# A two-layer decoder trunk in one core: weight sums, product order, buffers and transfers rescheduled by hand

## The chip, the cores and the metric

The kernel runs on one core of a Trainium2 chip. The metric is the device time of one execution in microseconds, the median of several runs; lower is better. The engines have short names in the profile: PE (TensorE, matmuls and transposes), PEld (its weight loads), DVE (VectorE), ACT (ScalarE), POOL (GpSimd), SP (SyncE). SP and POOL issue nearly all DMAs here.

## The reference, cut to what matters

The input x has 512 rows of 2048 columns, all float32. Layer 0 is forgetting attention (FoX) with 16 heads of 128, layer 1 is retention with 8 heads of 256 (keys) and 512 (values). Each layer is one input projection, the mixer, a SiLU gate and one output projection, and then a LayerNorm.

```python
def fox_branch(x, w_in, b_f, q_gain, k_gain, w_out):
    proj = einsum('bsd,de->bse', x, w_in)            # 2048 -> 4*2048 + 16
    q, k, v, gate, f_logit = split(proj, ...)
    q, k = rms_norm(heads(q), q_gain), rms_norm(heads(k), k_gain)
    c = cumsum(log_sigmoid(f_logit + b_f), axis=1)
    s = q @ k.T * scale + c[query] - c[key]          # causal
    o = softmax(s) @ v
    return (o * silu(gate)) @ w_out
def retention_branch(x, w_in, w_out):
    q, k, v, gate = split(x @ w_in, ...)             # 2048 -> 2*2048 + 2*4096
    q, k = rotary(q), rotary(k) * 256 ** -0.5
    o = causal (q @ k.T * decay) @ v, per head       # written in chunks
    return (group_norm_heads(o) * silu(gate)) @ w_out
def reference(x, ...):
    h = x
    for i in range(2):
        y = fox_branch(h, ...) if i == 0 else retention_branch(h, ...)
        h = layer_norm(ALPHA * h + y, ln_gain[i], ln_bias[i])
    return h
```

## The kernel before

**Products.** A float32 product is made of three matmuls of rounded parts: each operand is split into a high part and the rest, and `mm3` (lines 284 to 288) adds high x high, high x low and low x high. `split` (279 to 282) makes the high part on ScalarE (L281) and the low part on VectorE (L282). Weights come from DRAM as `w_raw` or `w_q` and are split on the way into `w_h` and `w_l`, three buffers each.

**Units and blocks.** A weight matrix is cut into units: 18 wide ones (1024 output columns) and 16 narrow ones (512). A unit is a 2 x 2 block product in Strassen's manner with seven products, p1 to p7; the sums of the left sides are the forms `a11`, `s1`, `s2` and so on. The right sides are sums of weight quarters. p1, p5, p6 and p4 share a chain: the quarter loaded first is `w_q`, and each of p5, p6 and p4 adds another quarter to it (L470, VectorE), to be split after that. p7's sum is L466. A product of a wide unit has 4 blocks of 12 matmuls of 128 x 512. The tables `ORDER`, `FIRST`, `REST` and `EARLY` give the order of the products, `blocks_of` unrolls them; within a group of two products the blocks alternate. W4 (output projection of layer 0, first half) and N8 (queries and keys of the first retention head) are plain products; W4's order is the table `HELD`, twelve of its 32 blocks use the split made for the block ahead of them (same weights, other rows).

**The planner.** Everything is issued in an order that class `Order` (83 to 215) finds while the program is built. All blocks of all units stand in one line. In a slot (`slot`) the planner loads weights up to nine blocks ahead, adds and splits two to three blocks ahead, and issues the block's matmuls. Before it adds block j it has split all blocks before j. Then it lets tasks go on. A task is a Python generator that yields what its next step needs: time on VectorE and ScalarE (`dve`, `act`), buffers ("rings": `mmp`, two PSUM buffers for everything but weights' products; `tmp`, `in0`, `g0`, `k0` and so on). A step goes in a slot only if the debts of both engines stay under `LIMIT`, 4.8 and 4.0 us; a slot pays off 2.7 to 2.8 us. When a block needs a buffer or a form that is not there (`require`), the planner forces tasks, whatever the debts, and so puts long chains into all queues at once. I call that a forced turn. Each engine executes its own queue strictly in that order.

**Tasks.** FoX (`Pair`, from 838): a pair of heads is projected in a narrow unit (N0 to N7), `normed` scales and transposes queries and keys (transposes L892, copies L886 and L887), `head` has eight turns of scores (L286 to L288 on `qk_h`), softmax (L931 to L953), transposes of the probabilities (L967), their copies `pT` (L922), products with the values (L998), transposes of the result (L1008). In each turn a step first copies what the turn ahead produced, frees its PSUM buffer, and then issues the next products. Heads go one after another, by `fox["heads"]`; they share the buffers g0, g1, g2 and d0. `to_columns` normalizes and transposes layer 0's output (L1241, copies L1229 and L1231). Retention (`Head`): N8 to N15 project queries and keys, W6 to W13 values and gates; `attend` makes rope (L1323 to L1327), scores and decay (L1355), `retain` the products with the values, the group norm (L1413 to L1430), the scaling by it (L1433), the gate's transposes (L1437), copies (L1444, L1445) and stores of the forms for the output projection. Those are fetched again by `fetch_form` for W14 to W17. In a unit, `keep` copies the sum of p1 into the buffer k0, which is free when the gates of the head ahead have been transposed.

**Transfers.** Weights and forms are loaded from SP's queue. W5 and W17 are run in the order `EARLY`: p7's and p4's weights are summed by DMAs that accumulate, from GpSimd's queue. `sum_ahead` (L399 to L407) issues all of p7's, four loads on SP and four accumulations on GpSimd, when p5 is done; right behind them in W17, `last_gains` (L1509 to L1512) issues two loads of 1 MB each, the last LayerNorm's gain and bias spread over all partitions.

Of the kernel before, what the change touches and what calls it, by code (L numbers as in the profile page):

```python
# [17 lines left out]
P = 128  # L18
# [25 lines left out]
def blocks_of(n, *groups):  # L44

    return [(p, c) for g in groups for c in range(n) for p in g]


FIRST = (("p1",), ("p2",))
REST = (("p5",), ("p6",), ("p3", "p7"), ("p4",))  # L50
ORDER = (("p1", "p5"), ("p6",), ("p3", "p7"), ("p2", "p4"))
# [7 lines left out]
        + [(2, 0, c, m) for c in range(4) for m in range(2)] + [(1, 1, c, 1) for c in range(4)]  # L59
        + [(2, 1, c, m) for c in range(4) for m in range(2)])  # L60
# [8 lines left out]
RINGS = dict(mmp=2, tmp=4, st=3, q=4, **{t: 1 for t in "k0 k1 k2 in0 in1 g0 g1 g2 d0 b0 b1 b2".split()})  # L69


LIMIT = 4.8, 4.0
# [10 lines left out]
class Order:  # L83
# [46 lines left out]
    def each(self, forced, rank):  # L130
        went = False
        for task in list(self.tasks):
# [8 lines left out]
            if not forced and any(d + c > most and c for d, c, most in zip(self.debt, cost, LIMIT)):  # L141
                continue
# [10 lines left out]
    time = 0.0  # L153

# [9 lines left out]
    def push(self, block):  # L164
        self.line.append(block)
        while len(self.line) - self.at > 9:
            self.slot()
# [11 lines left out]
    def slot(self):  # L179
# [22 lines left out]
        b.multiply()  # L202
        self.step()
# [19 lines left out]
def trunk(ctx: ExitStack, tc: tile.TileContext, xq, x, fb_f, columns, wf_in, narrow, wide, ln_g, ln_b, rot, decay,  # L223
# [80 lines left out]
    class Unit:  # L304
# [3 lines left out]
        def __init__(self, w, n, sink, rows=True, u2="k0"):  # L308
# [8 lines left out]
            self.kept_w = {}  # L317
# [17 lines left out]
        def keep(self, what, bank):  # L335
            n = self.shape[2]
            if self.wide or what == "u2":
                tag = {"p1": "k0", "p5": "k1", "u2": "k2"}[what] if self.wide else self.u2
# [27 lines left out]
        def after(self, p):  # L366
# [3 lines left out]
            if p == "p1":  # L370
                self.keep("p1", "x")
# [6 lines left out]
            if p == "p2":  # L378
# [20 lines left out]
        def sum_ahead(self):  # L399

            for i in range(2):
                t = pool.tile([P, 2, 2, 512], F32, name="v_sum", tag=HOME["s1"][i])
                for c in range(2):
                    self.summed["p7", 2 * i + c] = t[:, c]
                    d = t[:, c].rearrange("p a b -> p (a b)")
                    nc.sync.dma_start(d, self.source("12", 2 * i + c))
                    nc.gpsimd.dma_start(d, self.source("22", 2 * i + c), accum_op=ALU.add)  # L407
# [15 lines left out]
    class Block:  # L423
        before = None

        def __init__(self, unit, p, c, e, shares, shared, then_block, then_product):
# [15 lines left out]
            assert p != "p7" or shared or self.sums  # L442

# [139 lines left out]
    class PlainBlock:  # L583
        def __init__(self, unit, k, n, c, m, same, then, before, ahead):
            self.u, self.k, self.n, self.c, self.m = unit, k, n, c, m
            self.same, self.then, self.before, self.ahead = same, then, before, ahead
            self.done = False
            self.p = f"b{k}{n}"
# [119 lines left out]
    def fetch_form(i, name, tags, at=0, to=8):  # L708

        for c in range(at, to, 4):  # L710
            n = min(4, to - c)
            heads = 4 * i if i else c + n + (0 if name in ("a11", "a21", "s3") else 8)
            yield need(until=lambda: given[i > 0] >= heads and any(free[t] for t in tags))
# [10 lines left out]
            yield need(dve=dve(n * 256), act=act(n * 256), wait=3)  # L724
            split_form(name, t, c, c + n)
# [112 lines left out]
    class Pair:  # L838


        def __init__(self, i):
# [3 lines left out]
            self.rows_done = 0  # L845
# [20 lines left out]
        def normed(self):  # L866
# [10 lines left out]
            yield need(mmp=1, until=lambda: free["g0"] and free["g1"])  # L877
            take("g0")
            take("g1")
            self.qk = sb8("qk_h", "g0", F32R), sb8("qk_l", "g1", F32R)  # L880
            for s in range(ST + 1):
                if s:
                    yield need(act=0.85, dve=0.95, pe=0.45)
                    for i, gain in ((0, gq), (2, gk)):
                        h, l = (p[:, i:i + 2, (s - 1) * P:s * P] for p in self.qk)
                        nc.scalar.activation(h, t[:, i:i + 2], AF.Copy, scale=gain)  # L886
                        nc.vector.scalar_tensor_tensor(l, t[:, i:i + 2], gain, f32(h), op0=ALU.mult, op1=ALU.subtract)  # L887
                    give("mmp")
                if s < ST:
                    t = by4(mmp())  # L890
                    for h in range(4):
                        nc.tensor.transpose(t[:, h], raw[s][:, h * P:(h + 1) * P], ident)  # L892
# [5 lines left out]
        def head(self, i):  # L898
# [3 lines left out]
            yield need(d0=1, until=lambda: fox.get("forgot") and fox["heads"] == head)  # L902
            take("d0")
            cb = pool.tile([P, S], F32, name="cb", tag="d0")
# [5 lines left out]
            ps, p, tp = {}, {}, {}  # L910
            for t in range(8):
                wait = int(t > 0)
                if 5 <= t:
                    g = groups[t - 5]
                    yield need(act=sum(act(n_of(q)) for q in g), wait=wait, g2=int(t == 5))
                    wait = 0
                    if t == 5:
                        take("g2")
                        pT = sb8("pT", "g2")
# [20 lines left out]
                if 1 <= t < 4:  # L940
                    g = groups[t - 1]
                    yield need(act=sum(act(n_of(q)) for q in g), dve=sum(dve(n_of(q)) + 0.28 for q in g), wait=wait,
                               tmp=1)
                    wait = 0
                    b, at = tmp("p"), 0
# [12 lines left out]
                if t == 3:  # L958
                    give("d0")
                if 4 <= t < 7:  # L960
                    yield need(pe=0.45, wait=wait, mmp=1)
                    g = groups[t - 4]
                    tp[g] = by4(mmp())
                    at = 0
                    for q in g:
                        for k in range(q + 1):
                            nc.tensor.transpose(tp[g][:, at], p[q][0][:, k * P:(k + 1) * P], ident)  # L967
                            at += 1
                    give("tmp")
                if t < 3:  # L970
                    yield need(pe=0.7, wait=wait, mmp=1)
                    c, at = mmp(), 0
                    for q in groups[t]:
                        m = max(n_of(q), 256)
                        ps[q] = c[:, at:at + m]
                        at += m
                        mm3(ps[q], [x[:, i, q * P:(q + 1) * P] for x in self.qk], [x[:, 2 + i, :m] for x in self.qk],
                            True, True)
                    if t == 2:
                        if i:  # L980
                            give("g0")
                            give("g1")
                        else:
                            fox["heads"] = head + 1
# [14 lines left out]
            give("g2")  # L999
# [188 lines left out]
    def to_columns(m):  # L1188
# [24 lines left out]
        made = {}  # L1213
        for i in range(len(turns) + 2):
            yield need(dve=1.5 if m == 0 else 0.5, act=1.5, pe=0.45, mmp=int(i == 0))
            if 0 <= i - 2 and m == 0:
                s, c = turns[i - 2]
                es = slice(s % 2 * P, (s % 2 + 1) * P)
                k = c % 2 * 4
                split_form(f"a1{c // 2 + 1}", made.pop(i - 2), k, k + 4, es, s % 2 == 1)  # L1220
            if 0 <= i - 1 < 8:
                s, c = turns[i - 1]
                es = slice(s % 2 * P, (s % 2 + 1) * P)
                d = aq[f"{m + 1}{c // 2 + 1}"][:, c % 2 * 4:c % 2 * 4 + 4, es]
                for j in range(4):
                    k = c * 4 + j
                    g, b = cols[:, 2 + k:3 + k], cols[:, 2 + KT + k:3 + KT + k]
                    if j % (4 if m else 2) == 1:
                        nc.vector.tensor_scalar(d[:, j], ps[:, j], g, b, op0=ALU.mult, op1=ALU.add)  # L1229
                    else:  # L1230
                        nc.scalar.activation(d[:, j], ps[:, j], AF.Identity, scale=g, bias=b)  # L1231
                give("mmp")
                made[i - 1] = d
                if m and s % 2:
                    there.add((f"2{c // 2 + 1}", c % 2))
            if i < 8:
                s, c = turns[i]
                zs = z_part(s, c // 2)[:, c % 2 * 512:(c % 2 + 1) * 512]
                ps = by4(mmp())
# [347 lines left out]
```

## Time and profile before

| what | value |
|---|---|
| median of 3 runs | 2693.91 us (2693.76 to 2699.8) |
| profiled execution, its own time | 2688.65 us |
| its span, first to last instruction | 2686.9 us |
| mean granted clock of TensorE | 0.961 |
| busy: TensorE, VectorE, ScalarE, GpSimd | 2395.3, 1964.9, 1256.2, 212.4 us |
| moved by DMA | 482.71 MB, mean 180 GB/s |
| W4 and W5 (from the timeline) | 839 to 1105 us |
| retention's projections, N8 to W13 | 1105 to 2260 us |
| output projection, W14 to W17 | 2260 to 2660 us |

A wait in the profile names the instruction that waited, what ended the wait, the total in us, how often and the longest. In the timeline a row has start, duration, engine, line, operation, and in brackets the idle time of the engine ahead of it and what ended that. A row of the windows view has the busy time of each engine in a stretch, the granted clock (1.00 is full), the mean busy share of the 16 DMA engines and GB/s.

### The profile page before, as it was taken

Reading aid. Unit: us, or ns where it says so; the run is one execution under the profiler, and the core shown is the slowest. Engines: PE = TensorE matmul, PEld = TensorE weight load, DVE = VectorE, ACT = ScalarE, POOL = GpSimd, SP = SyncE. Lnnn points to the kernel's source line nnn. Section 1 sums busy time; section 2 is a strip of 40 time slices with the busy share of each in tenths; the row PEclk is TensorE's granted clock in tenths of the full one; section 3 lists DMA queues with packets and bytes.
Section 4 is the critical chain, followed back from the end, with each engine's and each line's share of the span. In section 5 each row is a group of like instructions: output and inputs, shape, how many; then the busy total and the mean of one; then the engine's idle time right before and its main releaser. Section 6 shows DMA issues by size and latency. Waiting matters only on the chain.

```text
span 2686.9 us, 34465 instructions
## 1 busy us (share of the span) xinstructions
PE 2395.3 (89%) x12964; PEld 2022.5 (75%) x12964; DVE 1964.9 (73%) x2551; ACT 1256.2 (47%) x1879; POOL 212.4 (8%) x316
## 2 busy tenths in 40 slices
PE   8889998998999697887889999999999998799975
PEld 8687787797798476776769797979797876577754
DVE  4768777667666255767778787878787878678758
ACT  4445566556556433553344444454444454434421
POOL 0000200110110101000010101010101010100010
PEclk9999999999999798999999999999999999899987
DMA  5344664664655368444465656565656566668682
GB/s 183 133 158 162 185 193 135 192 186 141 174 167 169 90 200 248 167 145 138 160 188 186 192 186 184 184 184 188 189 192 184 188 174 222 169 230 274 197 256 95
DMA packets 194487, 482.71 MB, mean 180 GB/s; under 512 B 19328, under 2 KB 71680, under 8 KB 194064
## 3 DMA queue, kind: packets, MB, share of 16 engines
q1 hardware_dynamic: 161872, 404.46, 45.5%
q0 software_dynamic: 32448, 76.04, 12.0%
q8 instruction: 102, 1.67, 0.2%
q14 instruction: 65, 0.53, 0.1%
HBM read 410.67 MB, written 69.76 MB: 179 GB/s over the span
## 4 chain that ended last, share of the span: by engine, by line
PE 26%; DVE 21%; ACT 7%; DMA 6%; issue 5%; SPq 0%; ACTq 0%; DVEq 0%
PE acc L287 8%; PE acc L286 8%; PE acc L288 8%; DVE w_l L282 7%; ACT w_h L281 5%; DVE w_q L470 5%; DMA w_raw<-in_wide 4%; DMA y_raw<-y_a 1%; DVE w_raw L466 1%; PE mmp L287 1%; PE mmp L288 1%; PE mmp L286 1%; DMA y_raw<-y_s 1%; DVE rope L1323 1%; DVE s L282 1%
## 5 line engine op out<-in xcount | busy, mean ns | idle before, releaser
L281 ACT ACTIVATE w_h<-w_q 128x1024 fp32r<-128x1024 f32 x384 | 403.4, 1058 | 665.3 <-DVE w_q L470 507.2
L282 DVE TENSOR_TENSOR w_l<-w_q,w_h 128x1024 fp32r<-128x1024 f32 x384 | 469.2, 1223 | 272.6 <-ACT w_h L281 269.9
L286 PE MATMUL acc<-w_h,s 128*128 128x512 f32 (+1 forms) x1536 | 575.9, 375 | 71.5 <-ACT w_h L281 48.6
L287 PE MATMUL acc<-w_l,s 128*128 128x512 f32 (+1 forms) x1536 | 576.5, 375 | 37.7 <-DVE w_l L282 37.3
L288 PE MATMUL acc<-w_h,s 128*128 128x512 f32 (+1 forms) x1536 | 564.2, 367 | 0.0
L286 PE MATMUL acc<-w_h,a 128*128 128x512 f32 (+1 forms) x1408 | 511.2, 363 | 37.3 <-ACT w_h L281 22.4
L282 DVE TENSOR_TENSOR w_l<-w_raw,w_h 128x1024 fp32r<-128x1024 f32 x324 | 394.4, 1223 | 203.1 <-ACT w_h L281 201.8
L287 PE MATMUL acc<-w_l,a 128*128 128x512 f32 (+1 forms) x1408 | 507.0, 360 | 3.6 <-DVE w_l L282 3.6
L281 ACT ACTIVATE w_h<-w_raw 128x1024 fp32r<-128x1024 f32 x324 | 339.3, 1054 | 358.2 <-DVE w_raw L466 183.2
L288 PE MATMUL acc<-w_h,a 128*128 128x512 f32 (+1 forms) x1408 | 505.3, 359 | 0.0
L286 PEld LDWEIGHTS acc<-w_h,s 128*128 128x128 f32 x1536 | 298.2, 194 | 129.6 <-ACT w_h L281 55.5
L287 PEld LDWEIGHTS acc<-w_l,s 128*128 128x128 f32 x1536 | 298.0, 194 | 115.3 <-DVE w_l L282 74.0
L470 DVE TENSOR_TENSOR w_q<-w_q,w_raw 128x1024 f32<-128x1024 f32 x280 | 341.7, 1220 | 35.2 <-DMA w_raw<-in_wide 32.4
L288 PEld LDWEIGHTS acc<-w_h,s 128*128 128x128 f32 x1536 | 298.0, 194 | 43.1
L286 PEld LDWEIGHTS acc<-w_h,a 128*128 128x128 f32 x1408 | 270.8, 192 | 77.5 <-ACT w_h L281 24.0
L287 PEld LDWEIGHTS acc<-w_l,a 128*128 128x128 f32 x1408 | 270.7, 192 | 45.1 <-DVE w_l L282 9.3
L288 PEld LDWEIGHTS acc<-w_h,a 128*128 128x128 f32 x1408 | 270.1, 192 | 38.3 <-DVE a L282 0.2
L286 PE MATMUL acc<-a,w_h 128*128 128x256 f32 x464 | 133.1, 287 | 10.6 <-ACT qk_raw L1298 10.4
L288 PE MATMUL acc<-a,w_l 128*128 128x256 f32 x464 | 132.3, 285 | 1.2 <-DVE w_l L282 1.2
L287 PE MATMUL acc<-a,w_h 128*128 128x256 f32 x464 | 132.1, 285 | 0.0
L286 PE MATMUL acc<-s,w_h 128*128 128x256 f32 x448 | 127.4, 284 | 3.1 <-ACT p L351 3.1
L288 PE MATMUL acc<-s,w_l 128*128 128x256 f32 x448 | 127.6, 285 | 0.1
(204 smaller groups left out, 2969.2 us busy)
## 6 DMA issues: line engine op xcount, KB each, us to landing
w_raw<-in_wide SPq DMA_DIRECT2D x360, 512.0 KB, 3.5
w_raw<-in_narrow SPq DMA_DIRECT2D x164, 512.0 KB, 3.5
w_q<-in_wide SPq DMA_DIRECT2D x68, 512.0 KB, 4.5
w_q<-in_narrow SPq DMA_DIRECT2D x28, 512.0 KB, 5.3
y_s<-ny POOLq DMA_DIRECT2D x48, 256.0 KB, 6.2
y_s<-y POOLq DMA_DIRECT2D x40, 256.0 KB, 4.1
y_raw<-y_s SPq DMA_DIRECT2D x32, 256.0 KB, 4.4
y_raw<-y_a SPq DMA_DIRECT2D x26, 256.0 KB, 4.6
```

Source lines behind the costliest of these rows:

```text
L281: nc.scalar.activation(h, src, AF.Copy)
L282: nc.vector.tensor_sub(l, src, f32(h))
L286: nc.tensor.matmul(ps, a[0], b[0], start=start, stop=False, skip_group_check=True)
L287: nc.tensor.matmul(ps, a[0], b[1], start=False, stop=False, skip_group_check=True)
L288: nc.tensor.matmul(ps, a[1], b[0], start=False, stop=stop, skip_group_check=True)
L466: nc.vector.tensor_add(self.t, self.t, u.lent.pop(("p3", c)))
L470: nc.vector.tensor_add(u.chain[c], u.chain[c], t)
L1323: nc.vector.tensor_mul(a, raw[j], cos[:, None, :].to_broadcast([P, 2, 512]))
```

## The change

1. **Sums ahead.** A block now has `follows`: the place in the line of the block that the same chain was last summed for (p1 for p5, p5 for p6, p6 for p4). Before a sum the planner splits only up to that block, not all blocks before it. So the sum of the next block comes ahead of the split of one that is waiting for its own high part. In `ORDER` p5 is written "+p5".
2. **TensorE's part first.** In `normed`, `head`, `to_columns`, `attend` and `retain` a step issues the next transposes or products ahead of the copies of what is there, if a `mmp` buffer is free at that moment; if not, after them, as before.
3. **Last pair.** Pair 7 has queries, keys, probabilities and the gate's row in buffers of its own (those of the forms s2, s4, s1), no longer in g0, g1, g2, d0.
4. **Orders.** The first wide unit and the first retention head take p2 ahead of p1 (`FIRST`), with other PSUM banks (`first_banks`). In `HELD` the second column half's blocks with m = 1 go to the end, and eight blocks instead of twelve use the split ahead.
5. **Transfers.** `sum_ahead` issues one DMA per slot; `last_gains` issues eight loads of 256 KB on GpSimd's queue, one per slot, from the end of p2. Forms fetched into g buffers come eight columns at a time instead of four, and s1, s2, s4 of layer 0 wait for all 16 heads.
6. **Limits.** 4.4 and 3.8 instead of 4.8 and 4.0, and 2.4 for ScalarE in the slot of p6's last block. In `to_columns` VectorE takes one of four copies in both halves.

```diff
-FIRST = (("p1",), ("p2",))
+FIRST = (("p2",), ("p1",))
-ORDER = (("p1", "p5"), ("p6",), ("p3", "p7"), ("p2", "p4"))
+ORDER = (("p1", "+p5"), ("p6",), ("p3", "p7"), ("p2", "p4"))
...
-LIMIT = 4.8, 4.0
+LIMIT = 4.4, 3.8
...
-            while self.split < self.added:
+            while self.split <= self.line[self.added].follows:
                 self.split_one()
             self.debt[0] += self.line[self.added].add()
...
+        self.most = (LIMIT[0], 2.4) if b.p == "p6" and b.last else LIMIT
...
+        def follows(self):
+
+            p = {"p5": "p1", "p6": "p5", "p4": "p6"}.get(self.p)
+            return -1 if p is None or self.sums or self.again else self.u.of[p, self.c].at
...
-                    nc.sync.dma_start(d, self.source("12", 2 * i + c))
-                    nc.gpsimd.dma_start(d, self.source("22", 2 * i + c), accum_op=ALU.add)
+            def steps():
+                for c in range(4):
+                    d = self.summed["p7", c].rearrange("p a b -> p (a b)")
+                    yield need()
+                    nc.sync.dma_start(d, self.source("12", c))
+                    yield need()
+                    nc.gpsimd.dma_start(d, self.source("22", c), accum_op=ALU.add)
+
+            spawn(steps(), 0)
...
+            self.tags = HOME["s2"] if i == 7 else ("g0", "g1")
+            self.tag_p = HOME["s4"][0] if i == 7 else "g2"
+            self.tag_c = HOME["s1"][0] if i == 7 else "d0"
...
+                if products:
+                    holds = full or t >= 5
+                    yield need(pe=0.6, wait=wait, mmp=int(not holds))
+                    wait = 0
+                    ahead = free["mmp"] and free["tmp"] >= full
+                    if ahead:
+                        b = tmp("p") if full else None
+                        products(t)
...
+                if products and not ahead:
+                    yield need(wait=0, mmp=1)
+                    products(t)
...
-            self.vg_unit.tags = dict(x=a, y=b, z=b)
-            banks[:] = c, b, a
-            return c, c
+            self.vg_unit.tags = dict(x=a, y=b, z=c)
+            banks[:] = b, c, a
+            return c, b
...
-            nc.sync.dma_start(gb[i], (ln_g, ln_b)[i][1:2, :].to_broadcast([P, D]))
+        for c in range(4):
+            cs = slice(c * 512, (c + 1) * 512)
+            for t, src in zip(gb, (ln_g, ln_b)):
+                yield need()
+                nc.gpsimd.dma_start(t[:, cs], src[1:2, cs].to_broadcast([P, 512]))
...
-    Unit(wide, 17, sink).run(EARLY, then={0: lambda s=steps: spawn(s(), 1), "p5": last_gains,
+    Unit(wide, 17, sink).run(EARLY, then={0: lambda s=steps: spawn(s(), 1), "p2": lambda: spawn(last_gains(), 0),
```

VectorE's queue in unit W16, in p6, before. The numbers tell buffers apart: a sum (L470) writes a `w_q` buffer, a split (L282) reads it.

```order
L470 TENSOR_TENSOR w_q_20379<-w_q_20379,w_raw_20557 128x1024
L282 TENSOR_TENSOR w_l_20692<-w_q_20379,w_h_20691 128x1024
L470 TENSOR_TENSOR w_q_20429<-w_q_20429,w_raw_20605 128x1024
L282 TENSOR_TENSOR w_l_20713<-w_q_20429,w_h_20712 128x1024
L470 TENSOR_TENSOR w_q_20472<-w_q_20472,w_raw_20648 128x1024
```

The same place now:

```order
L498 TENSOR_TENSOR w_q_20380<-w_q_20380,w_raw_20560 128x1024
L289 TENSOR_TENSOR w_l_20667<-w_q_20513,w_h_20666 128x1024
L289 TENSOR_TENSOR s3_20528<-y_raw_20529,s3_20527 128x1024
L498 TENSOR_TENSOR w_q_20427<-w_q_20427,w_raw_20608 128x1024
L289 TENSOR_TENSOR w_l_20690<-w_q_20380,w_h_20689 128x1024
L498 TENSOR_TENSOR w_q_20470<-w_q_20470,w_raw_20649 128x1024
```

Before, a split stands right behind the sum that it reads (20379, 20379); now another sum stands between them (20380, 20427, then the split of 20380).

TensorE's queue in W8, from the last matmuls of the fourth block of p1 to the first of p5's next block, before (a unit's matmuls are `acc`, the group norm's gates are `gate` or `p`):

```order
L288 MATMUL acc<-w_h,a_9286 128x512
L1437 MATMUL mmp<-ident,gate 128x128 x4
L286 MATMUL acc<-w_h,s_10019 128x512
L287 MATMUL acc<-w_l,s_10019 128x512
L288 MATMUL acc<-w_h,s_10020 128x512
```

and now:

```order
L295 MATMUL acc<-w_h,a_9333 128x512
L1521 MATMUL mmp<-ident,p_11439 128x128 x8
L293 MATMUL mmp<-qk_h 128x512
L294 MATMUL mmp<-qk_l,qk_h 128x512
L295 MATMUL mmp<-qk_h,qk_l 128x512
L293 MATMUL acc<-w_h,s_10072 128x512
L294 MATMUL acc<-w_l,s_10072 128x512
```

One set of four transposes stood between the two blocks; now there are two sets and, behind them, the next head's first scores (in which L293 to L295 come twice).

SP's queue in W17, before:

```order
L458 DMA w_raw<-in_wide 128x1024 x3
L406 DMA v_sum<-in_wide 128x1024 x4
L1512 DMA ln_last<-in_ln_g 128x2048
L1512 DMA ln_last<-in_ln_b 128x2048
L458 DMA w_raw<-in_wide 128x1024 x7
```

and now:

```order
L486 DMA w_raw<-in_wide 128x1024 x5
L424 DMA v_sum<-in_wide 128x1024
L486 DMA w_raw<-in_wide 128x1024 x2
L424 DMA v_sum<-in_wide 128x1024
L486 DMA w_raw<-in_wide 128x1024 x2
L424 DMA v_sum<-in_wide 128x1024
L486 DMA w_raw<-in_wide 128x1024
```

The four loads of p7's sums no longer stand together ahead of seven weight loads, and the gains are gone from SP's queue: they are the last loads of GpSimd's, behind its accumulations.

More of the change, by code (lines that the diff above doesn't have):

```diff
@@ L140, in each @@
             cost = n.get("dve", 0), n.get("act", 0)
-            if not forced and any(d + c > most and c for d, c, most in zip(self.debt, cost, LIMIT)):
+            if not forced and any(d + c > most and c for d, c, most in zip(self.debt, cost, self.most)):
                 continue
@@ L153 @@
     time = 0.0
+    most = LIMIT
     def require(self, met):
@@ L164, in push @@
     def push(self, block):
+        block.at = len(self.line)
         self.line.append(block)
@@ L369, in after @@
             cost = dve(2 * self.shape[2])
-            if p == "p1":
+            if p == "p2" and "p1" not in k:
+                self.keep("p2", "y")
+                self.leave("y")
+            elif p == "p1" and "p2" in k:
+                nc.vector.tensor_add(k["p2"][0], k["p2"][0], b["x"])
+                o.debt[0] += cost
+                self.hand(0, 0, "p2")
+            elif p == "p1":
                 self.keep("p1", "x")
@@ L942, in head @@
                     yield need(act=sum(act(n_of(q)) for q in g), dve=sum(dve(n_of(q)) + 0.28 for q in g), wait=wait,
-                               tmp=1)
-                    wait = 0
-                    b, at = tmp("p"), 0
+                               tmp=int(not (products and ahead)))
+                    wait = at = 0
+                    if not (products and ahead):
+                        b = tmp("p")
                     for q in g:
@@ L958, in head @@
                 if t == 3:
[L959 to L984, printed above, removed]
+                    give(d0)
+                if products and not ahead:
+                    yield need(wait=0, mmp=1)
+                    products(t)
                 if t in (5, 6):
@@ L1343, in attend @@
             ps, t = {}, {}
[L1344 to L1363 removed]
+            n = lambda k: S - k * P
```

237 lines of the change are left out of this document (150 added, 87 removed).

## The prediction

> **What bounds the kernel now.** I read the page first: the busy shares, the slices, the chain that ended last.
>
> ```profile
> span 2686.9 us, 34465 instructions
> PE 2395.3 (89%) x12964; PEld 2022.5 (75%) x12964; DVE 1964.9 (73%) x2551; ACT 1256.2 (47%) x1879; POOL 212.4 (8%) x316
> PEclk9999999999999798999999999999999999899987
> PE 26%; DVE 21%; ACT 7%; DMA 6%; issue 5%; SPq 0%; ACTq 0%; DVEq 0%
> ```
>
> TensorE is busy 89% of the span. No edit takes a matmul away, so all that can be won lies in the other 291.6 us (2686.9 - 2395.3), and in the slices where the clock digit is under 9. VectorE is on the chain for 21%, though it is busy less than TensorE: there are stretches where it serves TensorE too late. So next I read whom TensorE waited for.
>
> ```profile
> PE acc L286 <- ACT w_h L281: 71.1, 19, 18.3
> PE acc L287 <- DVE w_l L282: 40.9, 76, 1.3
> PE acc L286 <- ACT qk_raw L1298: 10.4, 1, 10.4
> PE acc L286 <- DVE z L1158: 4.4, 1, 4.4
> ```
>
> The columns are total us, times, longest. There is no single culprit: one wait of 18.3, one of 10.4, and 76 small ones. Each has its own place and its own edit, and I cost them one by one. A measurement of this kernel can tell about 0.3% from no change, 8 us. The terms are subtracted from the profiled execution (2688.65 us, span 2686.9). It ran 5.3 under the median 2693.91, so the same difference is then put on the median.
>
> **1. Sums one block ahead of splits.** A wide block at full clock is 12 matmuls of a stretch without idle time:
>
> ```profile
> 2530.00:2563.00 33.00, 33.00 (x147) 27.34 (x146) 30.27 (x34) 11.97 (x12) 0.00 (x0) 1.00 0.53 180
> ```
>
> 33.00/147 is 0.224 us each, 2.69 a block. Unit 16, part p6, shows what such a block costs where the chain is serial (timeline of DVE, ACT, PE):
>
> ```profile
> 2488.26 1.22 DVE L470 TENSOR_TENSOR w_q<-w_q,w_raw 128x1024 f32<-128x1024 f32 x1
> 2489.57 1.06 ACT L281 ACTIVATE w_h<-w_q 128x1024 fp32r<-128x1024 f32 x1 [1.57 <-DVE w_q L470]
> 2490.66 1.23 DVE L282 TENSOR_TENSOR w_l<-w_q,w_h 128x1024 fp32r<-128x1024 f32 x1 [1.19 <-ACT w_h L281]
> 2491.81 1.22 DVE L470 TENSOR_TENSOR w_q<-w_q,w_raw 128x1024 f32<-128x1024 f32 x1
> 2491.94 0.50 PE L287 MATMUL acc<-w_l,s 128*128 128x512 f32 x1 [0.50 <-DVE w_l L282]
> 2495.49 0.50 PE L287 MATMUL acc<-w_l,s 128*128 128x512 f32 x1 [0.48 <-DVE w_l L282]
> ```
>
> Sum, high half, low half follow each other with VectorE idle for 1.19 in the middle; from sum to sum 3.55 (2491.81 - 2488.26), and 3.55 between TensorE's two waits. With the next sum in that hole the period is VectorE's own 1.22 + 1.23 = 2.45, under 2.69. So such a block wins 3.55 - 2.69 = 0.86. Of the 76 waits on w_l, 37 lie in p5 and p6 blocks in which the order really changes (in p1/p5 alternation the mark "+p5" yields the same sequence). 37 x 0.86 = 32. VectorE has only 0.24 to spare in such a period and runs tasks as well, so I take three quarters: **-24** (bounds 0 and -32).
>
> **2. TensorE's part first in the FoX heads.** The waits of 120 to 881 us, and the granted clock of a part of it:
>
> ```profile
> PE mmp L892 <- DVE qk_l L887: 13.1, 12, 2.3
> PE mmp L967 <- ACT pT L922: 9.2, 4, 3.0
> PE mmp L286 <- DVE sm L953: 8.6, 5, 2.5
> PE mmp L1008 <- ACT o L1004: 4.0, 5, 1.0
> PE mmp L286 <- ACT pT L922: 2.0, 3, 1.5
> 250.00:500.00 250.00, 227.56 (x1367) 195.96 (x1366) 179.19 (x274) 148.46 (x304) 32.85 (x51) 1.00 0.57 174
> ```
>
> These 36.9 us are waits for a PSUM buffer that copies of the same step free. Now products go ahead if one of the two buffers is free when the step is planned; following the planner's rules, 72 of the 96 head products do. 36.9 x 0.75 = **-28** (bounds 0, if the copies are late anyway, and -37). The clock there is 1.00: no clock to win.
>
> **3. Fourth unit, out projection.** In W4 one block's second column half no longer comes early and waits for z L1158: 4.4 by its row, and a restart at half clock as in term 6, -6; the split is made again for it, in slots with room. The forms s1, s2 and s4 are fetched only after the last head, which W5 asks for a whole unit later: 0. Pair 7 gets its own buffers, but its heads still start only when the pair ahead has done its scores:
>
> ```profile
> PE mmp L967 <- DVE sm L953: 11.4, 4, 5.8
> ```
>
> (881 to 1019 us). I take -2 of these (bounds 0, -10). Together **-8**.
>
> **4. DMA-bound stages.** W5 at 1034 us, W17 at 2577 us, by stretch (last columns: clock, DMA share, GB/s), the queue of SP, landing times, and ScalarE:
>
> ```profile
> 1034.00:1047.00 13.00, 7.80 (x25) 5.72 (x24) 3.68 (x3) 3.17 (x3) 2.61 (x3) 0.74 1.06 276
> 1047.00:1060.00 13.00, 9.38 (x28) 6.85 (x27) 9.04 (x9) 4.23 (x4) 0.86 (x1) 0.74 1.03 312
> 2591.00:2609.10 18.10, 0.05 (x1) 0.06 (x1) 1.30 (x2) 1.06 (x1) 1.78 (x3) 0.56 1.05 296
> 2609.10:2624.00 14.90, 14.44 (x54) 11.38 (x55) 10.02 (x9) 6.16 (x7) 1.72 (x2) 0.84 0.96 272
> 2624.00:2640.00 16.00, 16.00 (x72) 13.28 (x71) 14.08 (x22) 9.04 (x9) 0.00 (x0) 1.00 0.21 67
> 2579.79 0.89 SPq L1512 DMA_DIRECT2D ln_last<-in_ln_g  x1
> 2581.50 36.36 SPq L458 DMA_DIRECT2D w_raw<-in_wide  x7
> ln_last<-in_ln_b SPq DMA_DIRECT2D x1, 1024.0 KB, 22.0
> 2607.94 1.06 ACT L281 ACTIVATE w_h<-w_q 128x1024 fp32r<-128x1024 f32 x1 [23.20 <-DVE w_q L470]
> ```
>
> Four sums of 512 KB and two gains of 1 MB were put ahead of the weights at once. At 296 GB/s with share 1.05 those 4.2 MB take 14.2 us, and the four accumulations on GpSimd's queue (2.1 MB) share the same engines; TensorE does almost nothing from 2591.0 to 2609.1, and at clock 0.84 after that loses 0.16 x 14.9 = 2.4. From 2624 the share is 0.21. The gains now come behind all weights, into that empty time: 2.1 MB, 7.1 us. The sums go one per slot: 4.2 MB in 8 slots of 2.7 is 194 GB/s beside weights at 180 (the row of term 1), 78 over the 296: in 21.6 us the backlog grows by 1.7 MB, 6 us, which the weights' lead of two to three blocks mostly takes. I leave 3 of the 18.1 + 2.4: **-17** (bounds -7 and -20). On GpSimd's queue an accumulation waits for its copy, and weights behind it wait too; that is in the 3 that I leave. W5 has the sums and no gains: TensorE is idle 5.2 + 3.6 in its two stretches, and loses 0.26 x 26 = 6.8 by the clock at most; about half of the 15.6 goes, **-8** (bounds 0, -14).
>
> By bytes alone W17 would win the 7.1 and the 2.4, 9, and W5 nothing; that is rival B's first half. The Trainium skill speaks for it (DMA: Bandwidth & Descriptors, Issuing engines are not separate DMA queues): DMAs of all issuing engines run on the same 16 engines, and spreading them saves only issue time. The shares of 1.05 agree with it; by it the sum would be 16 smaller.
>
> **5. First unit of layer 2, forms.** The 10.4 before N8's output block (a bank still being copied, L1298) goes, since p2 opens another bank; ScalarE, busy with forms, is late next: **-7** (bounds 0, -12). In W16 a form waits for its data at the head of ScalarE's queue (3.14 us in front of TensorE); forms are now fetched eight blocks at a time where it was four, so the second half is there when its split comes: **-4** with a restart at half clock (bounds 0, -6). W14's forced turns, 16 before and after by the planner's rules, come in two places instead of three, one restart fewer: **-4** (bounds -20, +10). In the turn to columns between the layers the copies are shared out otherwise, and the chain of copies stays as long: 0 (bounds -5, +5).
>
> ```profile
> 2519.98 0.50 PE L286 MATMUL acc<-w_h,s 128*128 128x512 f32 x1 [3.14 <-ACT w_h L281]
> ```
>
> **6. What gets worse.** The limits fall to 4.4 and 3.8. In W8, W10 and W12 the group norm's step then no longer fits in its slot, the buffer k0 is not free at p1.3, and the planner forces it: gate transposes (L1521) stand in TensorE's queue behind the norm, rope and a split. W8 shows two sets of transposes and scores there, where before one set stood. Before, this happens at W14 and, small, at W7:
>
> ```profile
> 2306.21 1.12 PE L1437 MATMUL mmp<-ident,p 128*128 128x128 f32 x4 [6.17 <-ACT p L1433]
> 2306.20:2310.10 3.90, 3.89 (x12) 3.26 (x13) 0.96 (x1) 0.00 (x0) 0.66 (x1) 0.51 0.93 222
> 1377.43 0.66 PE L1437 MATMUL mmp<-ident,gate 128*128 128x128 f32 x4 [2.42 <-ACT gate L1433]
> 1377.50:1381.00 3.50, 3.50 (x12) 2.89 (x13) 2.74 (x3) 0.69 (x1) 0.00 (x0) 0.60 0.93 173
> ```
>
> A large one costs 6.17 + 0.49 x 3.9 = 8.1, a small one 2.42 + 0.40 x 3.5 = 3.8. Three heads with one of each: 3 x 11.9 = **+36** (bounds 0, by the two split blocks in stock, and +60, if the large one's two sets cost 8.1 each).
>
> The row of 2.42 is followed by a clock of 0.60. The Trainium skill (TensorE: Matmul & The Clock Gate, What's actually happening) has the clock halve after an idle window of about 3.4 us; by that a small one would cost 2.4, and term 6 be 4 smaller. I go by the row.
>
> **Sum:** -24 - 28 - 8 - 17 - 8 - 7 - 4 - 4 + 36 = -64. Profiled 2625; on the median 2693.9 - 64 = 2630.
>
> **The rivals.** *A, slower.* The lower limits are the main effect: a task step that fitted at 4.8 is refused at 4.4 and forced later, with TensorE's queue behind it. I count 3 places. Eleven units have such steps (W1 to W3, W7 to W14); at 11.9 each all of them cost 131, 95 more than summed: 2725. From nine of them on (the 100 us of gains / 11.9 = 8.4) it is slower than before. For it: VectorE's 73%, and steps that the planner counts at 2.2 beside a slot's 2.45. Against: the planner's rules force only the ones named. *B, little.* Term 4 is a matter of bytes, W17 wins 9 and W5 nothing (+16); in the heads the copies set the pace and half of term 2 goes (+14), and term 5's 7 is taken by ScalarE: -64 + 37 = -27, 2667. For it: shares of 1.05. *C, more.* Forcing drains the debt early and TensorE has two blocks in stock, so term 6 is nothing, and term 1 is whole: -64 - 36 - 8 = -108, 2586. For it: DVE's 73%; against: the row of 6.17. That the change does not do what it says is true of "+p5" and of pair 7's gate, and is counted there.
>
> **How the numbers follow.** Forecast 0.50, A 0.12, B 0.22, C 0.16. Range: down past C's middle to 2578 (0.07 left out), up over B's bounds to 2692 (A's 0.11 left out). Faster by over 0.3% is under 2685.8: forecast, C and 0.17 of B, 0.83. Within: 0.05 of B, 0.01 of A, 0.06. Slower: 0.11.
>
> **What would show it.** Right: TensorE's waits on w_l fall from 76 to about 45; the wait of 18.3 is under 4, and ln_last lands after the last weights; L892's, L967's and sm's waits in the FoX stretch fall to a quarter; new waits of about 6 to 8 on L1521 at W8, W10 and W12 (about 1490, 1760 and 2030 us). Wrong: those waits missing (C), or standing at most units (A); the share at 1.0 with TensorE idle for over 8 us in W17 (B).

## The result, and the profile after

The changed kernel takes 2613.11 us (median of 4 runs, 2605.26 to 2620.05), the kernel before 2696.14 (4 runs). The ratio is 0.969, with a 95% interval of 0.9659 to 0.9721: about 83 us less. The profiled execution of the changed kernel happens to be its slowest, 2620.05 us, so the two traces differ by 68.6 us only (2686.9 to 2618.3). The page of the changed kernel begins with:

```profile
span 2618.3 us, 34343 instructions
PE 2372.2 (91%) x12964; PEld 2037.6 (78%) x12964; DVE 1962.9 (75%) x2547; ACT 1268.9 (48%) x1891; POOL 216.5 (8%) x324
PEclk9999999999999898998999999989999999899997
```

TensorE has the same 12964 matmuls; its idle time fell from 291.6 to 246.1 us (2618.3 - 2372.2). By stretches, from the first matmuls of their units in the two timelines:

| stretch | before | after | difference |
|---|---|---|---|
| start to N1 | 175.4 | 162.5 | -12.9 |
| N1 to N7, with W1 to W3 (FoX heads) | 663.6 | 629.1 | -34.5 |
| W4 and W5 | 265.6 | 255.3 | -10.3 |
| N8 and W6 | 165.7 | 156.5 | -9.2 |
| N9 to W13 (retention heads) | 990.0 | 1012.5 | +22.5 |
| W14 to the end | 426.6 | 402.4 | -24.2 |

The retention heads became slower, all else faster. TensorE's waits (total, times, longest) over the whole span:

```profile
PE mmp L1521 <- ACT p L1517: 47.9, 6, 13.9
PE acc L294 <- DVE w_l L289: 42.3, 35, 4.8
PE acc L293 <- ACT w_h L288: 25.9, 7, 9.1
```

The long wait on `w_h` is gone. Waits on `w_l` are half as many and some of them longer, so that their sum stayed (40.9 us before, 42.3 now). The new first row is the gate's transposes (L1437 before, L1521 now); its longest, 13.9 us, is at W14, where it was 6.17 before. In the FoX stretch, 120 to 835 us, of the 36.9 us of waits that term 2 was made of 9.2 remain. That is a quarter, a fall that the prediction named as a sign:

```profile
PE mmp L961 <- ACT pT L1003: 2.9, 3, 2.0
PE mmp L1068 <- ACT o L1064: 2.2, 3, 0.7
PE mmp L293 <- ACT pT L1003: 2.1, 2, 1.5
PE mmp L293 <- DVE sm L1035: 2.0, 2, 1.2
```

In W17 TensorE now waits 2.09 us where it waited 18.3. The windows (last columns: clock, DMA share, GB/s) and GpSimd's queue say why: the DMA engines are as full as before, but TensorE goes on. The gains are issued behind the last load of weights and take about 8 us to land, so most of them land while the share is still 0.93, and not in the emptier time at the end.

```profile
2540.00:2556.00 16.00, 15.07 (x64) 11.46 (x62) 7.82 (x8) 4.42 (x5) 2.60 (x3) 1.00 1.05 292
2556.00:2572.00 16.00, 13.25 (x57) 10.74 (x58) 13.78 (x19) 8.87 (x9) 5.27 (x9) 1.00 0.93 265
2572.00:2590.00 18.00, 12.55 (x53) 9.31 (x51) 17.13 (x39) 0.00 (x0) 2.17 (x4) 1.00 0.19 72
2544.68 1.06 POOL L529 DMA_DIRECT2D w_q<-in_wide  x1
2559.20 0.91 POOL L1600 DMA_DIRECT2D ln_last<-in_ln_g  x1
ln_last<-in_ln_g POOLq DMA_DIRECT2D x4, 256.0 KB, 8.3
```

And the forced turn in W8, in the timeline of PE, VectorE and ScalarE, with the clock behind it:

```profile
1440.83 1.12 PE L1521 MATMUL mmp<-ident,p 128*128 128x128 f32 x4 [9.94 <-ACT p L1517]
1431.78 0.16 DVE L1511 COPY gn_var<-gn_mv 128x2 f32<-128x2 f32 x1
1434.43 1.22 DVE L1390 TENSOR_TENSOR rope<-qk_raw,cos 128x1024 f32<-128x1024 f32 x1
1438.14 1.06 ACT L288 ACTIVATE qk_h<-rope 128x1024 fp32r<-128x1024 f32 x1 [8.06 <-DVE rope L1394]
1440.06 0.72 ACT L1517 ACTIVATE p<-p,gn_r 128x512 f32<-128x512 f32 x1
1440.90:1444.50 3.60, 3.60 (x11) 3.02 (x12) 1.15 (x2) 1.97 (x2) 1.29 (x3) 0.50 0.91 236
```

Group norm, rope, its high half, and only then the gate's scaling, for which TensorE's queue stands still 9.94 us. W10 and W12 have the same wait (9.94 and 9.93).

### The profile page after: what moved, and what is told of

Its sections match the earlier page's. It is cut to its first block, busy times and chain, and to the rows that moved or that the text cites. A ratio compares the mean times of both kernels' runs of the same rounds, so it can differ in the third digit from the quotient of the medians.

```text
span 2618.3 us, 34343 instructions
## 1 busy us (share of the span) xinstructions
PE 2372.2 (91%) x12964; PEld 2037.6 (78%) x12964; DVE 1962.9 (75%) x2547; ACT 1268.9 (48%) x1891; POOL 216.5 (8%) x324
## 4 chain that ended last, share of the span: by engine, by line
PE 28%; DVE 18%; DMA 7%; ACT 4%; issue 3%; SPq 0%; ACTq 0%; DVEq 0%
PE acc L294 8%; PE acc L293 8%; PE acc L295 8%; DVE w_l L289 7%; DMA w_raw<-in_wide 5%; DVE w_q L498 3%; ACT w_h L288 2%; DVE w_raw L494 1%; PE mmp L293 1%; PE mmp L294 1%; PE mmp L295 1%; DMA ln_g<-in_ln_g 1%; DVE rope L1390 1%; DVE s L289 1%; DMA y_raw<-y_a 0%
## 5 line engine op out<-in xcount | busy, mean ns | idle before, releaser
L294 PE MATMUL acc<-w_l,s 128*128 128x512 f32 (+1 forms) x1536 | 567.6, 370 | 38.5 <-DVE w_l L289 38.3
L293 PE MATMUL acc<-w_h,s 128*128 128x512 f32 (+1 forms) x1536 | 569.0, 370 | 26.6 <-ACT w_h L288 16.3
L295 PE MATMUL acc<-w_h,s 128*128 128x512 f32 (+1 forms) x1536 | 562.7, 366 | 0.0
L293 PE MATMUL acc<-w_h,a 128*128 128x512 f32 (+1 forms) x1408 | 512.6, 364 | 29.2 <-DVE p L403 10.8
L288 ACT ACTIVATE w_h<-w_raw 128x1024 fp32r<-128x1024 f32 x328 | 345.2, 1056 | 385.2 <-PE acc L295 124.5
L289 DVE TENSOR_TENSOR w_l<-w_raw,w_h 128x1024 fp32r<-128x1024 f32 x328 | 400.2, 1221 | 150.9 <-ACT w_h L288 144.7
L295 PE MATMUL acc<-w_h,a 128*128 128x512 f32 (+1 forms) x1408 | 505.3, 359 | 0.0
L293 PEld LDWEIGHTS acc<-w_h,s 128*128 128x128 f32 x1536 | 297.5, 194 | 75.7 <-ACT w_h L288 18.9
L498 DVE TENSOR_TENSOR w_q<-w_q,w_raw 128x1024 f32<-128x1024 f32 x280 | 340.1, 1220 | 17.0 <-DMA w_raw<-in_wide 13.9
L295 PEld LDWEIGHTS acc<-w_h,s 128*128 128x128 f32 x1536 | 297.2, 194 | 45.3
L293 PEld LDWEIGHTS acc<-w_h,a 128*128 128x128 f32 x1408 | 271.2, 193 | 68.9 <-issue 13.7
L295 PEld LDWEIGHTS acc<-w_h,a 128*128 128x128 f32 x1408 | 270.8, 192 | 38.6
L494 DVE TENSOR_TENSOR w_raw<-w_raw 128x1024 f32<-128x1024 f32 x88 | 107.4, 1221 | 75.5 <-DMA w_raw<-in_wide 69.5
L295 PE MATMUL acc<-a,w_l 128*128 128x256 f32 x464 | 133.5, 288 | 3.0 <-DVE w_l L289 3.0
L293 PE MATMUL acc<-a,w_h 128*128 128x256 f32 x464 | 133.7, 288 | 0.5 <-ACT w_h L288 0.5
L293 PE MATMUL acc<-s,w_h 128*128 128x256 f32 x448 | 127.3, 284 | 2.8 <-ACT p L358 2.8
```

The source lines that it names most:

```text
L288: nc.scalar.activation(h, src, AF.Copy)
L289: nc.vector.tensor_sub(l, src, f32(h))
L293: nc.tensor.matmul(ps, a[0], b[0], start=start, stop=False, skip_group_check=True)
L294: nc.tensor.matmul(ps, a[0], b[1], start=False, stop=False, skip_group_check=True)
L295: nc.tensor.matmul(ps, a[1], b[0], start=False, stop=stop, skip_group_check=True)
L494: nc.vector.tensor_add(self.t, self.t, u.lent.pop(("p3", c)))
```

## The experiments

All ratios are to the kernel before, in runs on the same chip; 0.001 is 2.7 us.

### Sums ahead of splits

*Taken out of the changed kernel.*

```diff
-            while self.split <= self.line[self.added].follows:
+            while self.split < self.added:
```

> The changed kernel with the old loop: all blocks ahead are split before a sum. Theory of term 1: 24 us more (37 blocks at 0.86, three quarters of them), 2630 to 2645, with TensorE's small waits on w_l back in p5 and p6. Rival: VectorE is kept by its tasks in these blocks anyway, and the sum's place is worth under 8 us, below 2621.

2717.16 us, ratio 1.0093 (1.0074 to 1.0111): 109 us more than the changed kernel, over four times my term, and slower than before. Both theories fall. I formed another: what counts is not TensorE's wait on `w_l`, but each hole in VectorE's queue, since all that stands behind it comes late.

*Alone, in the kernel before.* The edit is `follows` with its bookkeeping and nothing else; the planner's forced turns stay where they were.

> The kernel before with the first part of the change alone: a sum comes ahead of the splits that it does not need. Theory formed after the first four runs: every hole of 1.2 us in VectorE's queue counts, also where TensorE still has split blocks in stock, since the tasks behind it come late; the holes before w_l fall by some 100 us and the time by 50 to 100, to 2595 to 2645. Term 1 of the prediction, which counts only blocks in which TensorE itself waits: 24 us less, 2670.

2610.7 us, ratio 0.9697 (0.9675 to 0.9718): 82 us less. This one edit gives as much as the whole change. VectorE's rows for the low half of a sum (busy, mean ns, idle ahead of it), before, with the sums alone, and in the changed kernel without them:

```profile
L282 DVE TENSOR_TENSOR w_l<-w_q,w_h 128x1024 fp32r<-128x1024 f32 x384 | 469.2, 1223 | 272.6 <-ACT w_h L281 269.9
```
```profile
L283 DVE TENSOR_TENSOR w_l<-w_q,w_h 128x1024 fp32r<-128x1024 f32 x384 | 468.7, 1222 | 177.0 <-ACT w_h L282 173.9
```
```profile
L289 DVE TENSOR_TENSOR w_l<-w_q,w_h 128x1024 fp32r<-128x1024 f32 x384 | 468.8, 1223 | 293.8 <-ACT w_h L288 291.8
```

With the sums alone, 96 us of holes are gone. Ahead of the other low halves (`w_l` from `w_raw`) 76 more went (203.1 to 127.0 us), while the idle time ahead of the sums grew, p7's from 16.8 to 87.0 and the others' from 35.2 to 50.5: 86 us less over the four rows. ScalarE's idle time ahead of `w_h` from `w_q` fell too (665.3 to 503.6), so this run does not tell a filled hole on VectorE from a high half that comes earlier.

TensorE's own waits on `w_h` and `w_l` together fell by 26 us only (71.1 and 40.9 before, 19.1 and 67.0 here), about what term 1 had, out of 77.4 us between the two traces. The rest came elsewhere. The FoX stretch shows that the place of the sums costs time where TensorE did not wait on `w_l`: before, it waited 3.6 us on it there (6 times), and the sums alone shorten the stretch by 27.8 (663.6 to 635.8). More than half of that are waits on copies, though products and copies stand in the old order in this kernel:

```profile
PE mmp L901 <- DVE qk_l L896: 4.5, 8, 1.2
PE mmp L976 <- ACT pT L931: 4.4, 4, 1.2
PE mmp L287 <- DVE sm L962: 8.1, 5, 2.1
```

The first was 13.1 before, the second 9.2, the third 8.6; with the two other rows of term 2, 36.9 became 21.1.

*VectorE's time by itself.* The base is the changed kernel with the group norm's step at 1.9 (below, 2579 us).

```diff
             split(raw, *self.w)
+            if p == "p2" and u.wide and not u.early and u.n not in (0, 6):
+                nc.vector.tensor_sub(self.w[1], raw, f32(self.w[0]))
```

> The changed kernel with the group norm's step at 1.9 (2579 us) and, in addition, in the 52 blocks of p2 in W1 to W3 and W7 to W16 VectorE computes the low half twice: 63 us more of VectorE's time, which the planner doesn't count. If VectorE's time counts wherever it is spent, 40 to 63 us more, above 2619. If it counts only where VectorE is behind (p5, p6 and the tasks around them) and p2 and p4 have room, under 10 us, below 2589.

2606.77 us, 0.968 (0.9667 to 0.9693), 26 us more for 63.7 of VectorE. Between the two theories: a microsecond of VectorE costs 0.4 even in a place where it seemed to have room. Half of this is direct: the second low half is written into the same tile, and TensorE waits 13.2 us for it (14 times), so the edit is not a pure test of VectorE's time.

### TensorE's part first

```diff
-                    ahead = free["mmp"] and free["tmp"] >= full
+                    ahead = False
```

and in `normed` the transposes behind the copies.

> The changed kernel, in which the FoX heads and the scaling of queries and keys issue the copies first and the products behind them, as before. Theory of term 2: 28 us more, 2635 to 2648, all of it between N1 and W4. Rival (B): the copies set the pace of a head, and the order is worth half or less, 2613 to 2627.

2615.51 us, 0.9717 (0.9696 to 0.9737): 7 us more by the ratios, whose intervals overlap. The rival is right; whether the order is worth anything in the whole kernel is not shown by this run. The same edit beside the one that takes the sums out:

> The changed kernel without its first part and with the copies first in the FoX heads (both edits of the runs before together). If the two are additive: 2717 + 2 to 7, about 2720. If the order of products and copies is worth more where sums come late: 2730 or more. If it is worth nothing there: 2717 or less.

2725.28 us, 1.0123 (1.0103 to 1.0142), 8 more than without the sums alone. The FoX stretch by itself is 629.1 us with both parts of the change, 640.2 without the order, 659.3 without the sums, 670.5 with neither: the order is worth 11 there and the sums 30, and they add up.

### Transfers

```diff
+            for c in range(4):
+                d = self.summed["p7", c].rearrange("p a b -> p (a b)")
+                nc.sync.dma_start(d, self.source("12", c))
+                nc.gpsimd.dma_start(d, self.source("22", c), accum_op=ALU.add)
...
+            nc.sync.dma_start(gb[i], (ln_g, ln_b)[i][1:2, :].to_broadcast([P, D]))
```

> The changed kernel with the old transfers: the eight sum DMAs at once and the two loads of 1 MB on SyncE's queue behind them, in W17, and the sums at once in W5. Theory of term 4: 17 us more in W17 and 4 to 8 in W5, 2634 to 2638, with a wait of 15 to 18 us at p6 of W17. Rival (B, bytes alone): 9 us more, all in W17, 2622.

2624.03 us, 0.975 (0.9731 to 0.9769), 16 us more. With the first half of this edit alone (sums at once, gains late):

> The changed kernel (ratio to the kernel before 0.969) with the eight sum DMAs issued at once in W5 and W17, while the loads of the last gain and bias stay late and on GpSimd's queue. If only the bytes that come late count (rival B), this loses nothing: within 4 us of the changed kernel. If the spreading counts as in term 4, W17 loses 8 to 10 and W5 4 to 8: ratio 0.973 to 0.976.

2617.68 us, 0.9729 (0.9708 to 0.9751), 10 us more; the intervals don't quite part it from its neighbours. TensorE's longest wait on `w_l`, with all the old transfers and with the sums at once:

```profile
PE acc L294 <- DVE w_l L289: 67.7, 34, 19.3
```
```profile
PE acc L294 <- DVE w_l L289: 65.0, 38, 9.7
```

Both of these longest waits are in W17; in the changed kernel the wait there is 2.09. So the gains (later, on another queue and in smaller pieces, which no run parts) and the spreading of the sums each take about half of it. Bytes alone (rival B) don't explain it. W17 itself took 102.6, 95.0 and 85.3 us (84.9 to 89.6 over the seven traces with the new transfers and the sums ahead).

### Limits

```diff
-                yield need(dve=2.2)
+                yield need(dve=1.9)
```

> The changed kernel (median 2613 us), in which the planner counts the group norm's step at 1.9 us instead of 2.2, so that it fits under the lower limit and no turn is forced at W8, W10 and W12. Theory of term 6: the three waits of 9.9 us on L1521 and their restarts go, 25 to 36 us less, 2577 to 2588. Rival (C of the prediction): VectorE has that work to do in any case and the wait turns up as smaller ones in the same units, under 8 us less, above 2605.

2579.11 us, 0.9582 (0.9566 to 0.9599): 29 us less than the changed kernel; the three waits are gone. The limits alone, in the kernel before (`LIMIT = 4.4, 3.8`):

> The kernel before with the lower limits 4.4 and 3.8 alone. Term 6: forced turns at W8, W10 and W12 as in the changed kernel, 25 to 36 us more, 2718 to 2730. Rival: with the old loop VectorE has so many holes that the forced work fits in, under 8 us.

2749.22 us, 1.0207 (1.0187 to 1.0228): 56 us more, twice what I expected, with more and longer forced turns (this row was 6.6, 3, 6.2 before):

```profile
PE mmp L1437 <- ACT p L1433: 65.9, 9, 11.8
```

And the changed kernel with `LIMIT = 5.0, 4.0`:

> The changed kernel with limits 5.0 and 4.0 instead of 4.4 and 3.8: no turn is forced at W8, W10 and W12 nor at p1 of W7. If forced turns are all that the lower limits do, as much less as with the group norm's step made to fit, 2579, and some 4 us for W7: 2570 to 2582. Rival: higher limits let tasks delay the splits, and the time is above 2590.

2563.1 us, 0.9517 (0.9504 to 0.953): 47 us less than with 4.4 and 3.8, and under what I expected. Units without a forced turn changed too, most of them for the better (N3 53.1 to 45.8 us, N7 54.5 to 47.3, but W1 91.0 to 95.7). So forced turns in three heads are not all that the limits decide. The wait at W14 stays.

### p7's sum

The new loop also puts p7's sum ahead of splits. It then waits for its weights at the head of VectorE's queue (idle 75.5 us; 16.8 before):

```profile
L494 DVE TENSOR_TENSOR w_raw<-w_raw 128x1024 f32<-128x1024 f32 x88 | 107.4, 1221 | 75.5 <-DMA w_raw<-in_wide 69.5 <-DMA w_raw<-in_narrow 3.1 <-issue 2.8
```

In W8 of the kernel with the group norm at 1.9, the timeline of VectorE and TensorE, and the clock behind it:

```profile
1447.48 1.23 DVE L494 TENSOR_TENSOR w_raw<-w_raw 128x1024 f32<-128x1024 f32 x1 [3.38 <-DMA w_raw<-in_wide]
1448.62 2.57 DVE L289 TENSOR_TENSOR w_l<-w_raw,w_h 128x1024 fp32r<-128x1024 f32 x2
1449.89 0.50 PE L294 MATMUL acc<-w_l,s 128*128 128x512 f32 x1 [2.28 <-DVE w_l L289]
1449.90:1453.40 3.50, 3.50 (x11) 2.79 (x12) 1.23 (x1) 0.98 (x2) 0.00 (x0) 0.69 0.64 190
```

So I put p7's sums back behind the splits (`follows` is `self.at - 1` for p7):

> The changed kernel with the group norm's step at 1.9 (2579 us) and, in addition, the sums of p7 behind all splits ahead of them, as before; those of p5, p6 and p4 stay ahead. In the changed kernel p7's sum (L494) waits 75 us for its weights at the head of VectorE's queue, 17 before. Theory: the splits behind it are what TensorE waits for in p3 and p7 of W7 to W16, 2 to 5 us each and the clock after it, so 20 to 35 us less, 2545 to 2560. Rival: p7's sum ahead is part of the gain, and its wait for data falls into time in which TensorE has stock; then the same or 10 us more.

2572.33 us, 0.9547 (0.9534 to 0.9561): 9 us less, not 20. The sum's idle time fell to 19.5, the wait in W8 is gone, and W8 to W12 gain 1.9 to 3.7 us each; but in layer 1 W2 and W3 lose 2.5 each. (W17 took 4 longer, but its p7 is summed by DMAs, so the edit changes nothing there.) So, last, only in layer 2, with the higher limits:

> The changed kernel with limits 5.0 and 4.0 (2563 us) and, in the second layer alone, the sums of p7 behind all splits ahead of them. If the two gains are independent: W8 to W16 win some 1 to 3 us each as they did beside the group norm's smaller step, 8 to 15 in all, 2548 to 2557. Rival: the higher limits have already taken up the slack that p7's wait cost there, 2560 to 2566.

2541.61 us, 0.9439 (0.942 to 0.9457): 21 us less than the limits alone, and the best version. W9 to W12 take 84.1 to 84.4 us, against 86.6 to 89.2.

```profile
span 2543.0 us, 34367 instructions
PE 2346.8 (92%) x12964; PEld 2011.3 (79%) x12964; DVE 1959.2 (77%) x2547; ACT 1275.1 (50%) x1891; POOL 217.2 (9%) x324
```

## Why the prediction was right in its result, and wrong in two of its terms

The direction and the range held: 83 us less, where I had 64. That the sum came so near is in part luck: term 1 was 58 us too small, and terms 2 and 4 were 30 too large between them. The terms in order:

| term | predicted | measured | by |
|---|---|---|---|
| 1, sums ahead | -24 | -82 alone, -109 taken out last | runs alone and without |
| 2, TensorE's part first, FoX | -28 | -7 | run without |
| 4, transfers in W5 and W17 | -25 | -16 | run without |
| 6, lower limits | +36 | +29 (forced turns in three heads only), +47 against 5.0 and 4.0, +56 alone | three runs |
| 3 and 5, the rest | -23 | -7, or down to -25 | what is left over |

With -82, +29, -16, -7 and -7 the sum is -83; the last is only the remainder, its parts (pair 7, `HELD`, first unit, forms, and the order of products in the other tasks) were not tried. The limits cost 27 more where the sums come late (56 against 29), and the sums give 27 more where the limits are low (109 against 82), which would be one interaction, seen twice; with it the change without its sums is 56 - 16 - 7 - 7 = 26 slower, and it measured 25. But the 29 is the price of the forced turns in three heads and not of the limits: raised to 5.0 and 4.0 they gave 47, and the old 4.8 and 4.0 were not tried with the sums ahead. With 47 the remainder would be -25 and the limits' side of the interaction 9. So how the last two rows share the time stays open.

**Term 1.** The step that failed is "Of the 76 waits on w_l, 37 lie in p5 and p6 blocks in which the order really changes", multiplied by 0.86. The 0.86 was about right for such a block: the four blocks of p6 in W16 take 2.8 us each with the sums alone, and up to 3.56 before. But I counted only the blocks in which TensorE itself waited. A sum that comes late leaves a hole of 1.2 us ahead of a split and delays what stands behind it on VectorE, and TensorE meets that later, as a wait on a copy, on a kept sum, on a forced turn. The row that I needed was the profile page's: 269.9 us of VectorE's idle time ahead of `w_l`, not the 40.9 that TensorE waited. That the place of the sums costs time where TensorE has no wait on `w_l` is shown by the FoX stretch. That VectorE's holes and the tasks behind them are the way, and not ScalarE's earlier start, is argued from the waits that fell there.

**Term 2.** The step "These 36.9 us are waits for a PSUM buffer that copies of the same step free" was right as a reading and wrong as a cause. With the sums ahead, 16 of those 36.9 us went in the old order, so part of the copies were late because the sums were. The sign came true, a quarter of the waits is left, and the price did not: what the order adds is 11 us in the stretch and 7 in all, within the intervals. Terms 1 and 2 together were 52 and measured 89.

**Term 4.** Right in mechanism, W17 lost 17.3 us in the trace without it (102.6 against 85.3), as I had it. W5 took 109.5, against 108.0 in the changed kernel's trace, its slowest execution, and 104.9 and 105.3 in the traces of two other kernels with the new transfers (the group norm's step at 1.9, copies first): 2 to 5 us, where I had half of 15.6. The Trainium skill's rule (DMA: Bandwidth & Descriptors, Issuing engines are not separate DMA queues) holds in that the share stays at 1.05; but the order in which the bytes come was worth as much as their lateness.

**Term 6.** Places and kind were right: W8, W10 and W12, L1521. The wait is 9.94 with the clock at 0.50 for 3.6 us behind it, 11.7 a piece by itself, where I had 8.1 and a small one. Avoiding them gave 29, not 36. Rival C, which took them for hidden, is out; rival A had the right sign for the limits, and its many forced turns did not come. At W14, where I had a restart less, the wait doubled: it is 11.8 to 14.3 us in all traces but the two with the old limits (6.2 before, 5.0 with the sums alone). The raised limits don't take it away either (12.3), and why is open.

**What I did not see** is p7's sum: a sum ahead waits for its data with splits behind it, a wait that the change adds on VectorE's queue. Taking it away gave 9 and 21 us in the two runs, and it is in none of my terms.

## What to carry to other kernels

Where one engine feeds TensorE and runs other tasks in the same queue, look at the idle time of that engine ahead of the instruction, and not only at TensorE's wait on that one tile: the delay comes out elsewhere. Here 96 us of holes came with 82 us of time, and 63.7 us of added work cost 26, so the price of a microsecond has to be measured. A wait on a copy says that the copy was late, and not that its place in the queue was wrong. When instructions are moved ahead, look whether they wait for a DMA there, and when planner limits are lowered, count which steps no longer fit: both were found here in the order and one row of the profile, and the last kernel, with higher limits and p7's sums behind the splits in layer 2, gained 68 us more (0.969 to 0.9439).

## What was not expected of the hardware

The clock's answer to short waits is not a matter of their length alone. Behind 2.28 us without matmuls it was 0.69 for 3.5 us (W8 above), behind 2.42 in the kernel before 0.60; but in the kernel before two waits of 2.95 and 2.52 us, at 441 and 448 us, left it at full:

```profile
436.00:460.00 24.00, 18.46 (x88) 14.48 (x87) 18.95 (x28) 14.83 (x26) 0.00 (x0) 1.00 0.44 143
```

The Trainium skill (TensorE: Matmul & The Clock Gate, What's actually happening) calls the window of about 3.4 us free-running, and has the clock halve after an idle one. The traces agree on the grid: between changes the clock holds for multiples of 3.413 us. They don't agree that a whole window has to be idle. Cut along that grid, the window with the wait of 2.28 us had TensorE busy for 1.36 us, and the next one ran at half; the waits of 2.95 and 2.52 us are each cut in two by it, and no window there had less than 1.88 us of work:

```profile
1447.84:1451.25 3.41, 1.36 (x6) 1.14 (x7) 3.22 (x3) 2.01 (x2) 0.00 (x0) 1.00 0.18 52
1451.25:1454.66 3.41, 3.41 (x10) 2.63 (x9) 0.00 (x0) 0.00 (x0) 0.00 (x0) 0.50 0.79 263
439.52:442.94 3.42, 1.90 (x9) 1.21 (x7) 2.69 (x5) 1.79 (x6) 0.00 (x0) 1.00 0.51 153
446.35:449.76 3.41, 1.88 (x9) 1.06 (x7) 2.88 (x4) 2.85 (x5) 0.00 (x0) 1.00 0.68 217
```

In the fourteen traces of this case, the 406 falls of the clock all follow a window that was idle for at least 46%, and none of the 9446 windows after which it stayed full was idle for more than 57%. So the bound lies near half a window, as closely as the profile's modelled ends of matmuls show it.
